# Softmax of the attention scores over sample and prompt columns together: one 768-wide maximum and sum for each head

## The chip, the cores and the metric

The kernel runs on one core of a Trainium2 chip. The metric is device time in microseconds (us) of one execution, lower is better; the kernel before has a median of 1966.47 us in three runs (1965.4 to 1966.96). Engines are named as in the profile: PE (TensorE, matrix multiply), DVE (VectorE), ACT (ScalarE), POOL (GpSimd), SP (SyncE, which issues most transfers).

## The reference

A trunk of two layers. Each layer runs three token mixers on the same normalised input and merges them; sample (512 tokens) and prompt (256 tokens) are two independent sequences that share all weights, so attention never crosses from one to the other.

```python
def encoder_layer(x, c_act, ...):
    h = rmsnorm(x, g_pre) * (1 + scale) + shift
    z = h @ w_in                                      # 1024 -> 8864 columns
    o_a = mla_attention(cq, ckv, kr, ...)             # A: 8 heads, dense
    o_b = dilated_attention(rope(q), rope(k), v)      # B: 3 dilations x 4 heads, joined to 4
    o_c = neighbourhood_attention(q, k, v, rpb)       # C: 8 heads, window of 8 x 16 on a grid
    p_a = (o_a * silu(gate_a)) @ w_pa                 # the same for b, c
    mixed = mg[0] * p_a + mg[1] * p_b + mg[2] * p_c   # mg = sigmoid(merge)
    return x + gate * rmsnorm(mixed @ w_out, g_post)
# the middle of each attention
    p = softmax(q k^T * scale [+ bias, masked])
    o = p v
```

## The kernel before

**Layout.** Activations lie feature-major: partitions are features, the T = 768 columns are tokens, sample in columns 0 to 511 and prompt in 512 to 767 (GROUPS in the code). Matrix products run on operands split into a rounded `hi` and a rest `lo`, each in a 4-byte rounded type: ACT casts `hi`, DVE (sometimes POOL) subtracts to get `lo`, and PE multiplies with both.

**One head.** Scores are computed transposed: keys on the partitions, queries in the columns. The score tiles of a head are four `tq` tiles of 128 x 768 (128 keys each); the sample has four key tiles (columns 0 to 511 of all four), the prompt two (columns 512 to 767 of the first two). PE writes score parts to PSUM, ACT copies them (branch A, L647) or DVE adds bias and mask (branch C, L992 to L994; branch B, L825 and L830) into `tq`. The softmax needs a maximum and a sum over keys, that is over the tiles and over the partitions: DVE combines the tiles elementwise (L662, L664), and POOL reduces over the 128 partitions and hands the result to all of them (`partition_all_reduce`, L665; in branch B L853 and L868). Then DVE subtracts the maximum (L670), ACT exponentiates in place (L671), ACT and DVE make `hi` (L679) and `lo` (L680), and PE multiplies with the values (L683, into `o_ps`). The sum is reduced in the same way and sent to DRAM by SP (L672); it divides the output later (`row_gains`), so the multiplication with the values does not wait for it. All this stood once for the sample and once for the prompt: `soft_keys` is called for each of them in branches A and C, and branch B has its own loop (L840 to L869).

**Order.** Each engine works its instructions in the order of its own list. A list scheduler puts them in that order at build time and also decides when buffers are reused, so a change of a few instructions moves others. In the attention branches PE has other products to do between the heads' parts: projections of the layer's input that are needed later (`gate`, and `mg` for the merge). These are called fillers below. A head's scores go out, then some fillers, then the product with the values. PE in its order waits where the softmax of a head is not yet done.

**Buffers.** The scratch tiles of 512 columns come from a ring (`s`, 6 slots x 512, tiles given out in turn by `S()`); the softmax's tile of combined scores and its reduced result, the diagonal of `rows_of` (L226), branch C's bias tile `bp` and two tiles of the output projection (L1148) use it.

**Merge.** Behind branch C, `hi` and `lo` of the branches' outputs are made (`hi<-ox` on ACT at L247, `lo<-ox` through `sub_lo` at L160, on DVE, every third on POOL). The first of them already stand among the last heads of branch C. The library that POOL's `partition_all_reduce` needs is loaded over anew when an elementwise operation has stood between two of them; the listed order shows such a load as a row `ISA` without operands.

Of the kernel before, what the change touches and what calls it, by code (L numbers as in the profile page):

```python
# [20 lines left out]
P = 128  # L21
D = 1024
KT = 8
# [43 lines left out]
def trunk_kernel(ctx, tc, x_t, c_row, c_col, w_ada0, w_ada, cols, w_a, w_feat, w_val, w_val2, w_uqk, w_qr, w_uv, w_pj, w_o,  # L67
# [12 lines left out]
    BUFS = dict(ta=8, tm=4, tq=8, wo=18, cv=14, gp=2, xt=3, ut=3, st=11, rp=5, go=5, f=1, dn=1)  # L80


    RINGS = dict(q=(4, 1024), wh=(4, NS), wl=(4, NS), s=(6, NS), wr=(3, 1024), z=(16, 4), z4=(4, 2 * KT), nv=(8, 12))
    SINGLE = dict(hm=2 * KT * T, pz=NPZ * 2 * NS, rope=2 * NS, ident=P, ones=P, mb=1152, col=depth * NCOL,
                  ada=depth * 48, ada2=depth * 96, gpost=depth * 16, ab=depth * KT * 4, row=P)
    ROUNDED = ("hm", "pz", "q", "wh", "wl")
# [139 lines left out]

    def rows_of(y, bc, eng=None, dg=None):

        dg = S() if dg is None else dg
# [33 lines left out]


    nc.sync.dma_start(out=col, in_=cols)
    zero = S()
    nc.vector.memset(zero, 0.0)
    for z2 in pz:
        for z in z2:
# [11 lines left out]
        return out  # L281

    spare = []
    wide = [part["rope"], part["mb"][:, :1024], part["s"][:, 2048:]]

    def ada_load(src, j, tag, rest, n):

# [290 lines left out]
    def branch_a(l, h_, h):  # L578
# [14 lines left out]
        for pr in range(4):  # L593
# [37 lines left out]
            for e in range(2):  # L631
                hd = (pr % 2) * 2 + e
                (qs, qrs), ka = qn[e], kn[e]
                prods = ((ka, qs), (kb[e], qs), (krs, qrs))
                tq = [U("tq") for _ in range(4)]
                for g, (o, n) in enumerate(GROUPS):
                    nk = n // P

                    for k0 in range(0, nk, 1 + g):
                        sp = SP()  # L640
                        for k in range(1 + g):
                            kc = slice(o + (k0 + k) * P, o + (k0 + k + 1) * P)
                            for j, (w, a) in enumerate(prods):
                                nc.tensor.matmul(sp[:, k * 256:k * 256 + n], w[:, kc], a[:, o:o + n],
                                                 start=(j == 0), stop=(j == 2))
                        for k in range(1 + g):
                            nc.scalar.copy(tq[k0 + k][:, o:o + n], sp[:, k * 256:k * 256 + n])  # L647
                for g, (o, n) in enumerate(GROUPS):
                    xs = [x[:, o:o + n] for x in tq[:n // P]]
                    soft_keys(xs, n, den_scr[l, pr, e, 0:1, o:o + n])  # L650
                    o_ps = ps_o.tile([P, NS], F32, tag="o", name="o_ps")[:, :n]
                    for k, x in enumerate(xs):
                        pv(x, [(o_ps, vslice(va, hd, o // P + k), lambda a: a)], k == 0, k == n // P - 1)
                    out_half(o_ps, o_t, e, [(lambda a: a[:, o:o + n], lambda a: a)])
            nc.vector.tensor_mul(o_t, o_t, row_gains(l, pr))
            finish_pair(l, pr, o_t, u)

    def soft_keys(xs, n, den):

        def across(op):  # L660
            out, red = (S(), S()) if n > 256 else halves(S())
            nc.vector.tensor_tensor(out, xs[0], xs[1], op=op)  # L662
            for x in xs[2:]:
                nc.vector.tensor_tensor(out, out, x, op=op)  # L664
            nc.gpsimd.partition_all_reduce(red, out, P, RED.max if op == ALU.max else RED.add)  # L665
            return red

        m = across(ALU.max)
        for x in xs:
            nc.vector.tensor_sub(x, x, m)  # L670
            nc.scalar.activation(x, x, AF.Exp)  # L671
        nc.sync.dma_start(out=den, in_=across(ALU.add)[0:1])  # L672

    def pv(x, terms, first, last):
# [113 lines left out]
    def branch_b(l, h, hl):  # L788
# [4 lines left out]
        for hd in range(4):  # L793
# [39 lines left out]
            for g, (o, n) in enumerate(GROUPS):  # L833
                nt = n // 128
                t0 = o // 128
                tbv = tbs[g]
                v1, v2 = (x.rearrange("p (s i) -> p s i", s=SB[g]) for x in tbv)

                def across(out, op):
                    nc.vector.tensor_tensor(strided(out[:, :n], g), v1, v2, op=op)  # L840
                    if g == 0:
                        nc.vector.tensor_tensor(out, out, tq[0][:, :NS], op=op)
                        for t in (1, 2):
                            ow = out[:, NW[t]:NW[t] + 256]
                            nc.vector.tensor_tensor(ow, ow, tq[1][:, (t - 1) * 256:t * 256], op=op)  # L845
                    else:
                        for w in wins:
                            nc.vector.tensor_tensor(out[:, :256], out[:, :256], w, op=op)

                mx = S()  # L850
                across(mx, ALU.max)
                m = S()
                nc.gpsimd.partition_all_reduce(m[:, :n], mx[:, :n], P, RED.max)  # L853
                if g == 0:
                    nc.vector.tensor_sub(tq[0][:, :NS], tq[0][:, :NS], m)
                    nc.vector.tensor_sub(two(tq[1][:, :NS]), two(tq[1][:, :NS]), win_ap(m))
                else:
                    for w in wins:
                        nc.vector.tensor_sub(w, w, m[:, :256])
                nm = strided(m[:, :n], g)  # L860
# [87 lines left out]
    def branch_c(l, h, hl):  # L948
        state["phase"] = "c"
        vcs = None  # L950
        for pr in range(4):
# [12 lines left out]
            for e in range(2):  # L964
# [3 lines left out]

                bm, bp = U("rp", name="bm"), S()
# [18 lines left out]
                for t in range(2):  # L990
                    edge = bm[:, 512 + t * P:640 + t * P]
                    nc.vector.tensor_add(tq[t][:, 0:P], sp[t][:, 0:P], edge)  # L992
                    nc.vector.tensor_add(tq[t][:, P:NS], sp[t][:, P:], bm[:, P - t * P:512 - t * P])
                    nc.vector.tensor_add(tq[t][:, NS:], sp[2][:, t * 256:t * 256 + 256], bp[:, t * 256:t * 256 + 256])  # L994
                for g, (o, n) in enumerate(GROUPS):
                    xs = [x[:, o:o + n] for x in tq]
                    soft_keys(xs, n, den_scr[l, 6 + pr, e, 0:1, o:o + n])
# [131 lines left out]
    def project(l, mixed, last):  # L1129
# [14 lines left out]
        for t in range(T // P):  # L1144
            g = int(t >= 4)
            c0 = t * P - GROUPS[g][0]
            xt = U("xt", name="xt"), S()
            x2, u2 = xt[1][:, :256], xt[1][:, 256:]  # L1148
# [263 lines left out]
```

## Time and profile before

| | before |
|---|---|
| median of 3 runs | 1966.47 us (1965.4 to 1966.96) |
| the profiled execution's own time, its span | 1966.35 us, 1964.6 us |
| busy: PE, DVE, ACT, POOL | 94%, 78%, 52%, 34% |
| mean granted clock of PE | 0.978 |
| `partition_all_reduce` at L665 | 128 instructions, 314.2 us |

"Busy" is the share of the span in which an engine works; the mean says little of a single stage. The stages in the span are: preparation to about 130 us, then in layer 0 branch A to 360, B to 600, C to 800, merge and output projection to 1060, and in layer 1 branch A from 1150, B from 1360, C from 1600 to about 1805, merge and output after it.

### The profile page before, as it was taken

The page shows a single profiled execution, that of the slowest core. Times are in us where ns is not written, and L with a number is a line of the kernel's source. Part 1 is how long each engine was busy: PE and PEld are TensorE (multiplying, and loading weights), DVE is VectorE, ACT ScalarE, POOL GpSimd, SP SyncE. Part 2 cuts the span into 40 slices and gives each one's busy share as a digit, 9 for nine tenths or more (in the row PEclk, how much of TensorE's full clock was granted, in tenths as well). Part 3 has the DMA queues.
Part 4 walks back from the last instruction along what each step waited for, and adds up shares of the span by engine and source line. Part 5 has one row for each costly group of instructions (what it writes and reads, how often), then busy time and mean ns, then how long its engine had stood idle before and what let it go on. Part 6 is the DMA issues. An engine that isn't in the chain of part 4 may idle for free. (4 is left out here: it accounts for less than half of the span.)

```text
span 1964.6 us, 30204 instructions
## 1 busy us (share of the span) xinstructions
PE 1845.0 (94%) x10674; PEld 1638.1 (83%) x10674; DVE 1530.9 (78%) x3018; ACT 1018.6 (52%) x2123; POOL 664.2 (34%) x432
## 2 busy tenths in 40 slices
PE   7897999999989987999999999999999999987998
PEld 6886888888877876888999888889888778876898
DVE  8957768579987999896587467687699868997763
ACT  5356556356577455322464356574566684653241
POOL 6404415202221454316534024253022212454570
PEclk9998999999999999999999999999999999998999
DMA  8432241232313233445452332422222222233652
GB/s 294 150 117 62 86 139 57 71 99 82 92 54 92 79 117 115 167 143 191 140 197 89 124 99 88 135 76 86 87 85 85 88 75 89 87 107 99 217 174 71
DMA packets 94904, 221.25 MB, mean 113 GB/s; under 512 B 18096, under 2 KB 32504, under 8 KB 94752
## 3 DMA queue, kind: packets, MB, share of 16 engines
q1 hardware_dynamic: 90144, 213.02, 33.4%
q10 hardware_dynamic: 4608, 6.29, 1.1%
q8 instruction: 84, 1.38, 0.3%
q14 instruction: 68, 0.56, 0.1%
HBM read 173.78 MB, written 28.18 MB: 103 GB/s over the span
## 5 line engine op out<-in xcount | busy, mean ns | idle before, releaser
L665 POOL PARTITION_ALL_REDUCE fixed<-fixed x128 | 314.2, 2486 | 496.3 <-DVE fixed L662 337.0
L201 PE MATMUL mg<-fixed 128*128 128x512 f32 (+1 forms) x2304 | 436.2, 342 | 1.4 <-DVE o_t L397 0.7
L201 PEld LDWEIGHTS mg<-fixed 128*128 128x128 f32 x2304 | 360.3, 191 | 51.6 <-PE sp L984 1.0
L177 ACT CAST fixed<-fixed 128x512 fp32r<-128x512 f32 (+1 forms) x332 | 199.5, 606 | 339.3 <-PE mg L201 117.8
L160 DVE TENSOR_TENSOR fixed<-fixed,fixed 128x512 fp32r<-128x512 f32 (+3 forms) x309 | 224.2, 729 | 113.9 <-ACT fixed L177 110.7
L201 PE MATMUL qkb<-fixed 128*128 128x512 f32 (+1 forms) x1152 | 211.9, 338 | 0.0
L201 PEld LDWEIGHTS qkb<-fixed 128*128 128x128 f32 x1152 | 177.0, 189 | 24.2
L201 PE MATMUL gate<-fixed 128*128 128x512 f32 (+1 forms) x960 | 184.0, 341 | 1.6 <-DVE tq L830 1.3
L201 PEld LDWEIGHTS gate<-fixed 128*128 128x128 f32 x960 | 150.0, 191 | 22.0 <-DVE tq L830 1.5
L1064 PE MATMUL pp<-hi,fixed 128*128 128x512 f32 (+1 forms) x640 | 161.5, 340 | 5.0 <-ACT th L1019 4.7
L680 DVE TENSOR_TENSOR fixed<-tq,fixed 128x512 fp32r<-128x512 f32 (+1 forms) x160 | 127.9, 821 | 2.7 <-ACT fixed L679 2.5
L1064 PEld LDWEIGHTS pp<-hi,fixed 128*128 128x128 f32 x640 | 111.9, 192 | 19.9 <-ACT th L1019 5.1
L671 ACT ACTIVATE tq<-tq 128x512 f32<-128x512 f32 (+1 forms) x160 | 83.4, 545 | 82.7 <-DVE tq L670 82.5
L429 POOL MEMSET kb<- 64x768 f32 x56 | 41.1, 736 | 209.5 <-PE sp L820 121.0
L670 DVE TENSOR_TENSOR tq<-tq,fixed 128x512 f32<-128x512 f32 (+1 forms) x160 | 97.8, 660 | 16.3 <-POOL fixed L665 16.2
L1163 PE MATMUL op<-wo,fixed 128*128 128x384 f32 (+1 forms) x648 | 108.2, 320 | 1.8 <-POOL wo L160 1.8
L1064 PE MATMUL pp<-lo,fixed 128*128 128x512 f32 (+1 forms) x320 | 108.9, 341 | 0.8 <-DVE lo L160 0.8
L1163 PEld LDWEIGHTS op<-wo,fixed 128*128 128x128 f32 x648 | 101.3, 188 | 3.2 <-POOL wo L160 3.1
L311 DVE SCALAR_TENSOR_TENSOR fixed<-tm,fixed 128x768 f32<-128x768 f32 (+1 forms) x128 | 93.3, 729 | 2.1 <-DMA tm<-in_w_ada_dram 0.4
L868 POOL PARTITION_ALL_REDUCE fixed<-fixed x16 | 49.0, 3084 | 128.4 <-DVE fixed L845 65.7
L662 DVE TENSOR_TENSOR fixed<-tq 128x256 f32<-128x256 f32 (+1 forms) x128 | 79.1, 623 | 14.3 <-ACT tq L647 10.8
L679 ACT CAST fixed<-tq 128x512 fp32r<-128x512 f32 (+1 forms) x160 | 80.8, 530 | 11.0 <-PE o_ps L683 8.2
(245 smaller groups left out, 3910.7 us busy)
## 6 DMA issues: line engine op xcount, KB each, us to landing
fixed<-in_w_feat_dram SPq DMA_DIRECT2D x108, 512.0 KB
th_scr<-the SPq DMA_DIRECT2D x35, 384.0 KB
th<-th_scr SPq DMA_DIRECT2D x35, 384.0 KB
tm<-in_w_ada_dram SPq DMA_DIRECT2D x32, 384.0 KB
fixed<-in_w_val_dram SPq DMA_DIRECT2D x20, 512.0 KB
xs<-xb SPq DMA_DIRECT2D x96, 96.0 KB
fixed<-in_w_pj_dram SPq DMA_DIRECT2D x32, 256.0 KB
fixed<-in_w_o_dram SPq DMA_DIRECT2D x16, 512.0 KB
```

The source lines that it names most:

```text
L160: eng.tensor_sub(out, a, b)
L177: nc.scalar.copy(hi[:, :m], raw[:, o:o + m])
L201: state["mm"] = nc.tensor.matmul(outs[g], w[:, wsl], a[g], start=(i == 0 and wi == 0), stop=(i == nk - 1 and wi == 2))
L311: nc.vector.scalar_tensor_tensor(junk, x, 1.0, c, ALU.mult, ALU.mult, accum_out=ada2[:, l, i, g, j:j + 1])
L662: nc.vector.tensor_tensor(out, xs[0], xs[1], op=op)
L665: nc.gpsimd.partition_all_reduce(red, out, P, RED.max if op == ALU.max else RED.add)
L670: nc.vector.tensor_sub(x, x, m)
L671: nc.scalar.activation(x, x, AF.Exp)
L679: nc.scalar.copy(hi, x)
L680: nc.vector.tensor_sub(lo, x, f(hi))
L1064: nc.tensor.matmul(pp, w[:, ws], o[k][a][:, o_:o_ + n], start=(i == 0), stop=(i == 3 * nk - 1))
L1163: mm = nc.tensor.matmul(op[cc], m[a][g][:, k, c0:c0 + P], parts[k][cc][b], start=(k == 0 and i == 0), stop=(k == KT - 1 and i == 2))
```

## The change

The maximum and the sum of a head are made once, over 768 columns: combined tile 128 x 768, one reduction over the partitions for the maximum, one for the sum. In branches A and C the subtraction and the exponential of the first two `tq` tiles are 768 wide, those of the last two 512. In branch B the combining and the subtraction stay in two parts (their windows differ), the exponentials are 768 wide, and both maxima are made before the first subtraction. The sum goes to DRAM in one transfer. The ring `s` has four slots of 768 columns (3072 columns as before), and its other users take the first 512 columns of a slot. In the changed kernel lines behind `soft_keys` are three or four further down: combining L665 and L667, reduction L668, subtraction L673, exponential L674, `hi` L682, `lo` L683, product with the values L686; branch B's reductions L851.

```diff
-    RINGS = dict(q=(4, 1024), wh=(4, NS), wl=(4, NS), s=(6, NS), wr=(3, 1024), z=(16, 4), z4=(4, 2 * KT), nv=(8, 12))
+    RINGS = dict(q=(4, 1024), wh=(4, NS), wl=(4, NS), s=(4, T), wr=(3, 1024), z=(16, 4), z4=(4, 2 * KT), nv=(8, 12))
...
+                soft_keys(tq, den_scr[l, pr, e, 0:1])
                 for g, (o, n) in enumerate(GROUPS):
                     xs = [x[:, o:o + n] for x in tq[:n // P]]
-                    soft_keys(xs, n, den_scr[l, pr, e, 0:1, o:o + n])
...
-    def soft_keys(xs, n, den):
+    def soft_keys(tq, den):
+
+
+        cols = (T, T, NS, NS)
 
         def across(op):
-            out, red = (S(), S()) if n > 256 else halves(S())
-            nc.vector.tensor_tensor(out, xs[0], xs[1], op=op)
-            for x in xs[2:]:
-                nc.vector.tensor_tensor(out, out, x, op=op)
+            out, red = S(), S()
+            nc.vector.tensor_tensor(out, tq[0], tq[1], op=op)
+            for x in tq[2:]:
+                nc.vector.tensor_tensor(out[:, :NS], out[:, :NS], x[:, :NS], op=op)
             nc.gpsimd.partition_all_reduce(red, out, P, RED.max if op == ALU.max else RED.add)
             return red
 
         m = across(ALU.max)
-        for x in xs:
-            nc.vector.tensor_sub(x, x, m)
-            nc.scalar.activation(x, x, AF.Exp)
+        for x, n in zip(tq, cols):
+            nc.vector.tensor_sub(x[:, :n], x[:, :n], m[:, :n])
+            nc.scalar.activation(x[:, :n], x[:, :n], AF.Exp)
         nc.sync.dma_start(out=den, in_=across(ALU.add)[0:1])
...
-                for x in tq:
-                    nc.scalar.activation(x[:, o:o + n], x[:, o:o + n], AF.Exp, scale=0.125)
-                sm = S()
-                across(sm, ALU.add)
-                dn = S()
-                nc.gpsimd.partition_all_reduce(dn[:, :n], sm[:, :n], P, RED.add)
-                nc.sync.dma_start(out=den_scr[l, 4 + hd // 2, e, 0:1, o:o + n], in_=dn[0:1, :n])
+            for x in tq:
+                nc.scalar.activation(x, x, AF.Exp, scale=0.125)
+            nc.sync.dma_start(out=den_scr[l, 4 + hd // 2, e, 0:1], in_=across(ALU.add)[0:1])
```

DVE's list at the first head of branch A, layer 0, before (`tq` are the score tiles, `fixed_73` the plain scratch, `fixed_72` the rounded scratch with `hi` and `lo`):

```order
L662 TENSOR_TENSOR fixed_73<-tq 128x512
L664 TENSOR_TENSOR fixed_73<-fixed_73,tq 128x512
L662 TENSOR_TENSOR fixed_73<-tq 128x256
L664 TENSOR_TENSOR fixed_73<-fixed_73,tq 128x512
L410 SCALAR_TENSOR_TENSOR qs<-qn_1721,qs 64x512
L410 SCALAR_TENSOR_TENSOR qs<-qn_1722,qs 64x256
L670 TENSOR_TENSOR tq<-tq,fixed_73 128x256 x2
L662 TENSOR_TENSOR fixed_73<-tq 128x256
L670 TENSOR_TENSOR tq<-tq,fixed_73 128x512 x4
L662 TENSOR_TENSOR fixed_73<-tq 128x512
L680 TENSOR_TENSOR fixed_72<-tq,fixed_72 128x512
```

The same place of the changed kernel:

```order
L665 TENSOR_TENSOR fixed_73<-tq 128x768
L410 SCALAR_TENSOR_TENSOR qs<-qn_1703,qs 64x512
L410 SCALAR_TENSOR_TENSOR qs<-qn_1704,qs 64x256
L667 TENSOR_TENSOR fixed_73<-fixed_73,tq 128x512 x2
L673 TENSOR_TENSOR tq<-tq,fixed_73 128x768 x2
L673 TENSOR_TENSOR tq<-tq,fixed_73 128x512 x2
L665 TENSOR_TENSOR fixed_73<-tq 128x768
L683 TENSOR_TENSOR fixed_72<-tq,fixed_72 128x512
```

The prompt's separate combining (128x256) and its two subtractions are gone into rows of 128x768, and two operations on `qs` (the next head's queries) stand inside the combining for the maximum instead of behind it.

POOL's list at the last heads of branch C, layer 1, before (an `ISA` row with sizes is a reduction, one without is a load of the library):

```order
L429 MEMSET kb 64x768 x2
L665 ISA fixed_73<-fixed_73 128x256
L665 ISA fixed_73<-fixed_73 128x512
L665 ISA fixed_73<-fixed_73 128x256
L160 ISA
L160 TENSOR_TENSOR lo<-ox,hi 128x768
L665 ISA
L665 ISA fixed_73<-fixed_73 128x512
L665 ISA fixed_73<-fixed_73 128x256
L665 ISA fixed_73<-fixed_73 128x512 x2
L665 ISA fixed_73<-fixed_73 128x256 x2
```

The same place of the changed kernel:

```order
L429 MEMSET kb 64x768 x2
L668 ISA fixed_73<-fixed_73 128x768 x2
L160 ISA
L160 TENSOR_TENSOR lo<-ox,hi 128x768
L668 ISA
L668 ISA fixed_73<-fixed_73 128x768 x5
```

Before, the `lo` stands behind the last sum of the sixth head and ahead of the seventh's maxima; now it stands between the sixth head's maximum and its sum.

PE's list at the second head of branch A, layer 0, before (`o_ps` are the products with the values, `sp` the scores, `gate` and `mg` the fillers):

```order
L683 MATMUL o_ps<-fixed_72,va 128x512 x8
L644 MATMUL sp<-qs,ka 128x256
L644 MATMUL sp<-qs,kb 128x256
L644 MATMUL sp<-qrs,krs 128x256
...
L683 MATMUL o_ps<-fixed_72,va 128x256 x4
L201 MATMUL gate_1798<-fixed_72 128x512 x22
L201 MATMUL gate_1799<-fixed_72 128x256 x22
L683 MATMUL o_ps<-fixed_72,va 128x512
```

The same place of the changed kernel, just ahead of that head's product with the values:

```order
L201 MATMUL mg_1841<-fixed_72 128x512
L201 MATMUL mg_1842<-fixed_72 128x256
L686 MATMUL o_ps<-fixed_72,va 128x512 x5
L686 MATMUL o_ps<-fixed_72,va 128x256
L686 MATMUL o_ps<-fixed_72,va 128x512 x3
L686 MATMUL o_ps<-fixed_72,va 128x256 x3
L201 MATMUL mg_1900<-fixed_72 128x512 x19
L201 MATMUL mg_1901<-fixed_72 128x256 x19
```

Now all 24 pairs of `gate` and the first 24 pairs of `mg` stand between this head's scores and its first `o_ps`; before, 22 pairs of `gate` did.

## Rows read from the trace of the kernel before

**Rows 1.** The page, part 1: busy time of each engine, share of the span.

```profile
PE 1845.0 (94%) x10674; PEld 1638.1 (83%) x10674; DVE 1530.9 (78%) x3018; ACT 1018.6 (52%) x2123; POOL 664.2 (34%) x432
```

**Rows 2.** PE's waits by line and releaser: us in total, times, longest.

```profile
PE o_ps L683 <- DVE fixed L680: 16.1, 16, 2.1
PE o_ps L683 <- ACT tq L647: 11.2, 1, 11.2
PE o_ps L683 <- ACT fixed L679: 8.4, 2, 6.1
```

**Rows 3.** Windows inside branch C, layers 0 and 1: PE, PEld, DVE, ACT, POOL busy; clock.

```profile
680.00:780.00 100.00, 88.83 (x502) 76.41 (x502) 97.46 (x172) 52.43 (x108) 53.89 (x26) 0.95 0.34 112
1690.00:1765.00 75.00, 66.16 (x379) 56.13 (x378) 71.96 (x125) 44.85 (x95) 37.80 (x19) 0.98 0.30 97
```

**Rows 4.** Window: branch A, layer 0, columns as in rows 3.

```profile
130.00:360.00 230.00, 209.60 (x1154) 181.99 (x1153) 173.46 (x288) 132.29 (x286) 88.29 (x38) 0.95 0.29 92
```

**Rows 5.** POOL's timeline, single reductions: start, us, line, [idle before, releaser].

```profile
663.96 1.73 POOL L665 PARTITION_ALL_REDUCE fixed<-fixed  x1
686.75 1.06 POOL L665 PARTITION_ALL_REDUCE fixed<-fixed  x1 [1.23 <-DVE fixed L662]
1354.54 3.24 POOL L665 PARTITION_ALL_REDUCE fixed<-fixed  x1 [7.84 <-DVE fixed L664]
1770.72 1.80 POOL L665 PARTITION_ALL_REDUCE fixed<-fixed  x1 [10.19 <-DVE fixed L662]
```

**Rows 6.** DVE's groups by line and shape: 680 to 780, 1690 to 1765, whole span.

```profile
L662 DVE TENSOR_TENSOR fixed<-tq 128x512 f32<-128x512 f32 x11 | 7.4, 683 | 0.0
L670 DVE TENSOR_TENSOR tq<-tq,fixed 128x256 f32<-128x256 f32 x8 | 3.0, 416 | 0.0
L460 DVE TENSOR_TENSOR xb<-xb,xs 128x768 f32<-128x768 f32 x24 | 22.9, 952 | 0.2
L680 DVE TENSOR_TENSOR fixed<-tq,fixed 128x512 fp32r<-128x512 f32 x96 | 87.5, 925 | 0.1
```

**Rows 7.** Timelines of POOL, DVE and PE at the first head of branch A, layer 0.

```profile
158.88 3.11 POOL L665 PARTITION_ALL_REDUCE fixed<-fixed  x2 [40.12 <-DVE fixed L662]
159.29 1.01 DVE L410 SCALAR_TENSOR_TENSOR qs<-qn,qs 64x512 fp32r<-64x512 f32 x2
162.68 3.39 DVE L670 TENSOR_TENSOR tq<-tq,fixed 128x512 f32<-128x512 f32 x4
169.01 1.28 DVE L680 TENSOR_TENSOR fixed<-tq,fixed 128x512 fp32r<-128x512 f32 x2
170.41 2.08 PE L683 MATMUL o_ps<-fixed,va 128*128 128x512 f32 x4 [11.16 <-ACT tq L647]
```

**Rows 8.** Timelines of PE, ACT and POOL at the last heads of branch C, layer 1.

```profile
1767.77 4.17 PE L201 MATMUL mg<-fixed 128*128 128x512 f32 x16
1767.90 0.83 ACT L247 CAST hi<-ox 128x768 fp32r<-128x768 f32 x1 [3.79 <-DMA ox<-o_scr]
1774.09 0.83 ACT L247 CAST hi<-ox 128x768 fp32r<-128x768 f32 x1
1780.53 1.84 POOL L160 TENSOR_TENSOR lo<-ox,hi 128x768 fp32r<-128x768 f32 x1 [8.02 <-DVE fixed L690]
1788.33 2.87 POOL L665 PARTITION_ALL_REDUCE fixed<-fixed  x2 [5.96 <-issue]
1793.12 0.58 PE L683 MATMUL o_ps<-fixed,vb 128*128 128x256 f32 x1 [6.08 <-ACT fixed L679]
```

**Rows 9.** Window at the last heads of branch C, layer 1, columns as in rows 3.

```profile
1789.00:1806.10 17.10, 9.18 (x28) 7.46 (x29) 15.90 (x23) 8.04 (x17) 11.34 (x5) 0.50 0.21 65
```

**Rows 10.** DVE and POOL timelines in branch C; durations of line L680, ns min/median/max.

```profile
1737.82 2.73 DVE L680 TENSOR_TENSOR fixed<-tq,fixed 128x512 fp32r<-128x512 f32 x1
1737.39 3.60 POOL L665 PARTITION_ALL_REDUCE fixed<-fixed  x1 [3.97 <-DVE fixed L662]
L680 DVE TENSOR_TENSOR fixed<-tq,fixed x160: 403/677/2753, 166.6 to 1816.8; 128x512 fp32r<-128x512 f32 x96, 128x256 fp32r<-128x256 f32 x64
```

More of the change, by code (lines that the diff above doesn't have):

```diff
@@ L227, in rows_of @@
     def rows_of(y, bc, eng=None, dg=None):
-        dg = S() if dg is None else dg
+        dg = S()[:, :NS] if dg is None else dg
         for t in range(y.shape[-1]):
@@ L265, in trunk_kernel @@
     nc.sync.dma_start(out=col, in_=cols)
-    zero = S()
+    zero = S()[:, :NS]
     nc.vector.memset(zero, 0.0)
@@ L283, in trunk_kernel @@
     spare = []
-    wide = [part["rope"], part["mb"][:, :1024], part["s"][:, 2048:]]
+    wide = [part["rope"], part["mb"][:, :1024], part["s"][:, 2048:3072]]
     def ada_load(src, j, tag, rest, n):
@@ L832, in branch_b, with across @@
             early(l, hl, FILL[l][9 + hd])
[L833 to L840, printed above, removed]
+            def across(op):
+                both, red = S(), S()
+                for g, (o, n) in enumerate(GROUPS):
+                    v1, v2 = (x.rearrange("p (s i) -> p s i", s=SB[g]) for x in tbs[g])
+                    out = both[:, o:o + n]
+                    nc.vector.tensor_tensor(strided(out, g), v1, v2, op=op)
                     if g == 0:
@@ L847, in across @@
                         for w in wins:
[L848 to L853, printed above, removed]
+                            nc.vector.tensor_tensor(out, out, w, op=op)
+                nc.gpsimd.partition_all_reduce(red, both, P, RED.max if op == ALU.max else RED.add)
+                return red
+            ms = across(ALU.max)
+            for g, (o, n) in enumerate(GROUPS):
+                v1, v2 = (x.rearrange("p (s i) -> p s i", s=SB[g]) for x in tbs[g])
+                m = ms[:, o:o + n]
                 if g == 0:
@@ L858, in branch_b @@
                     for w in wins:
-                        nc.vector.tensor_sub(w, w, m[:, :256])
-                nm = strided(m[:, :n], g)
+                        nc.vector.tensor_sub(w, w, m)
+                nm = strided(m, g)
                 nc.vector.tensor_sub(v1, v1, nm)
                 nc.vector.tensor_sub(v2, v2, nm)
-                for x in tq:
-                    nc.scalar.activation(x[:, o:o + n], x[:, o:o + n], AF.Exp, scale=0.125)
-                sm = S()
-                across(sm, ALU.add)
-                dn = S()
-                nc.gpsimd.partition_all_reduce(dn[:, :n], sm[:, :n], P, RED.add)
-                nc.sync.dma_start(out=den_scr[l, 4 + hd // 2, e, 0:1, o:o + n], in_=dn[0:1, :n])
+            for x in tq:
+                nc.scalar.activation(x, x, AF.Exp, scale=0.125)
+            nc.sync.dma_start(out=den_scr[l, 4 + hd // 2, e, 0:1], in_=across(ALU.add)[0:1])
+            for g, (o, n) in enumerate(GROUPS):
+                nt = n // 128
+                t0 = o // 128
+                tbv = tbs[g]
                 o_ps = ps_o.tile([P, NS], F32, tag="o", name="o_ps")
@@ L967, in branch_c @@
                 prods = ((ka, qs), (kb[e], qs))
-                bm, bp = U("rp", name="bm"), S()
+                bm, bp = U("rp", name="bm"), S()[:, :NS]
                 nc.scalar.dma_start(out=bm[:, 512:], in_=bias_s[l, hd])
@@ L994, in branch_c @@
                     nc.vector.tensor_add(tq[t][:, NS:], sp[2][:, t * 256:t * 256 + 256], bp[:, t * 256:t * 256 + 256])
+                soft_keys(tq, den_scr[l, 6 + pr, e, 0:1])
                 for g, (o, n) in enumerate(GROUPS):
                     xs = [x[:, o:o + n] for x in tq]
-                    soft_keys(xs, n, den_scr[l, 6 + pr, e, 0:1, o:o + n])
                     o_ps = ps_o.tile([P, NS], F32, tag="o", name="o_ps")
@@ L1147, in project @@
             xt = U("xt", name="xt"), S()
-            x2, u2 = xt[1][:, :256], xt[1][:, 256:]
+            x2, u2 = xt[1][:, :256], xt[1][:, 256:NS]
             xt = xt[0]
```

## The prediction

> **What bounds the kernel now.** I read the page first: PE is busy in 94% of the span, DVE in 78%, POOL in 34% [rows 1]. The change takes nothing from PE: it issues as many matrix products as before. So it can only win or lose in the waits of PE, and the second view is the list of those waits. Three of its lines belong to the softmax: PE stands before the product with the values until `lo`, the evacuation of scores or `hi` is there, 16.1 us in 16 pieces, 11.2 us in one, 8.4 us in two [rows 2]. Third I asked, stage by stage, which engine is full when PE waits. In branch A of layer 0 nothing is: PE works 209.60 of 230 us and DVE 173.46 [rows 4]; its losses sit at single places, above all at the first head. In the middle of branch C it is DVE: 97.46 of 100 us in layer 0 and 71.96 of 75 us in layer 1, while PE works 88.83 and 66.16 [rows 3]. There a shorter DVE list should shorten the span; elsewhere only a shorter chain from the last score to the first product with the values does.
>
> **POOL.** Single reductions, matched by the listed order to their sizes, took 1.73 us (maximum, 512), 1.06 (maximum, 256), 3.24 (sum, 512) and 1.80 (sum, 256) [rows 5]. The line through the two sizes gives 1.73 + 0.67 = 2.40 us for a maximum over 768 and 3.24 + 1.44 = 4.68 for a sum. A head so costs 7.08 instead of 7.83 us, and 160 reductions become 80: 40 heads x 0.75 = 30 us less on POOL. POOL is no bound by its busy share [rows 1], so none of it counts by itself. What counts is when a result is there: a head's maximum comes 2.40 - 1.73 = 0.67 us later than the sample's alone did, and when the sum of the head ahead stands in front of it on POOL, another 3.24 -> 4.68, 1.44 us later.
>
> **DVE.** In A and C a head loses four instructions: one 512- and one 256-wide operation become one of 768, once in the maximum, once in the sum, twice in the subtraction. Undisturbed, the three widths take 0.683, 0.416 and 0.952 us [rows 6], so a merge saves 0.147 us and a head 0.59 us. Over 32 heads that is 19 us, but it is worth time only where DVE is full: the windows of rows 3 hold 11 combinings of 512 (two to a head, 5.5 heads) and 8 subtractions of 256 (two to a head, 4 heads) [rows 6]. 9.5 heads x 0.59 = **-5.5 us**. Bounds: 0, if the freed time goes into other waits of PE, and -5.5 x 16/9.5 = -9 if all of branch C's 16 heads gain. In branch B DVE's count stays; there only exponentials are merged, on ACT, which is busy in 52% [rows 1] of the span, as in A and C: nothing. If ACT were full anywhere, its 96 merged exponentials would count there as DVE's merges do; its share of 52 and 60% in the windows of rows 3 excludes it.
>
> **DVE beside POOL.** A `lo` of 512 took 2.73 us while a reduction of 3.60 us had begun just before it; the median over all widths is 0.677 and the mean of the 512-wide is 0.925 [rows 6, 10]. So some operations are held up to 2.05 us, most not at all. The excess, 4 x 0.25 = 1 us a head, over 9.5 heads 9.5 us, falls by 10% if it goes with the reductions' time and by half if it goes with their number: -1 to -5; I take **-2 us**, nearer the first, since the sums, which run beside the `lo`s, keep their length. The Trainium skill, "SBUF — State Buffer", section "Who interferes with whom", says that a DVE instruction with two SBUF inputs and a GpSimd instruction that reads SBUF exclude one another for a whole instruction; the row of 2.73 us fits it, the median does not. What that rule would make of the sum is a rival below.
>
> **First head of A, layer 0.** PE waits 11.16 us for it with no filler at hand, and its order there is the same after the change [rows 7]. Before, POOL has both maxima at 158.88 + 3.11 = 161.99. After, the 768-wide combining needs the prompt's scores too. Their own combining, 0.42 long, and a last one of 0.68 stood ahead of 159.29 [rows 7], so they were there by 158.2; I take 157.7, since DVE was busy with the sample before. 157.7 + 0.95 + 1.01 (the `qs` pair [rows 7], which now stands inside) + 2 x 0.68 = 161.0, plus 2.40 = 163.4, 1.4 us later. The subtractions then take 2 x 0.95 + 2 x 0.68 = 3.3 instead of 3.39 [rows 7]. Cost: **+1.3 us**, between 0 and +3.
>
> **Other heads of A.** I counted in the order how much work PE has between a head's last score and its first product with the values, at 0.25 us per 512 columns (16 took 4.17 us [rows 8]) and half for 256. In layer 0 that was 3.4, 8.5, 12.9, 22.9, 8.4, 18.5, 11.9 and 23.5 us; after the change it is 3.4, 17.9, 17.8, 28.0, 20.0, 27.7, 24.8 and 22.4. In layer 1 the lowest four rise from about 15 to above 20. So the scheduler has put the fillers ahead of the products that waited. The chain needs, on idle engines, 2.3 (combining) + 4.68 + 2.40 (a sum ahead, the maximum) + 3.3 (subtractions) and four more steps of 512 columns (evacuation, exponential, `hi`, `lo`) at about 0.68 [rows 10] = 15.4 us at the worst: less than 17.8. A has half of the 32 heads that share the 16.1 us of waits for `lo` [rows 2], so up to 8; as C is fuller I take less than half of that, **-3 us**, between 0 and -8. In branch B PE has 14.7 to 24.9 us before and 22 to 28.9 after: nothing; without that cover each of 8 heads would pay its later results, 0.67 + 1.44 us.
>
> **Last heads of C, layer 1.** Before, POOL makes a `lo` between reductions: it starts at 1780.53 after 8.02 us of idleness, and the next reduction only at 1788.33, after 5.96 us in which POOL waits for nothing that shows [rows 8]; the order has a load of the library on either side. The seventh head's maxima are done at 1788.33 + 2.87 = 1791.20, PE then stands for 6.08 us [rows 8], and in the 17.1 us from 1789 PE works 9.18 at a granted clock of 0.50, 1.2 GHz [rows 9]. At 2.4 GHz without waits this work takes 4.6: 12.5 us lost. After, `lo` stands one step earlier, between the sixth head's maximum and sum. It needs its `hi`, before done at 1774.9 [rows 8]. Another `hi` waited 3.79 us for its operand from DRAM until 1767.90 [rows 8]. If the `hi` in question comes without such a wait, by 1764, POOL is free at 1764 + 6 + 1.84 + 6 = 1778, and 7.1 us later, at 1785, sum and maximum are done; if it stands two steps behind a wait as long as that one, at about 1772, they are done at 1793. I take the middle, 1789: **-2 us**, between -6 and, with half the clock lost for it, +4.
>
> **The rest.** 80 transfers of sums become 40, issued by SP; they serve the division of a pair of heads, off the path, and half of SP's waits for POOL go with them. The ring holds one head in either form (6 x 512, 4 x 768). The output projection's two uses of it need the slot of four token tiles back instead of six; a 256-column load is all that hangs on it: nothing.
>
> **Sum.** From the profiled execution's 1966.35 us (its span of 1964.6 and 1.75 around it; 0.12 below the median): -5.5 - 2 + 1.3 - 3 - 2 = -11.2, **1955 us**.
>
> **Rivals.**
> *Slower, 1976.* One reduction over 768 columns in place of two that could be passed by. POOL works in order, so the next head's maximum waits 4.68 + 2.40 = 7.1 us behind a sum, not 3.24 + 1.73 = 5.0. It decides where DVE's own queue, three quarters full in A [rows 4], stretches the 15.4 us chain beyond PE's 18 to 28: 2.4 us more are enough at the shortest. Ten such heads cost 21 us; against the gains of 11 that is +10. For it: at the first head the 768-wide form is later. Against: the longer covers.
> *No change, 1966.* The waits for the softmax go, but PE then stands for the keys' preparation and the outputs' evacuation, which the same full DVE makes; the gain in C is nothing, the one in A balances the first head.
> *Far faster, 1936.* The longer covers take away all waits for `lo` and `hi`: 16.1 + 8.4 [rows 2] = 24.5 us, of which the sum holds 5; 19 more. Against: in C the waits are DVE's, and it remains nearly full.
> *The exclusion for whole instructions, 1948.* DVE is stopped whenever POOL reduces: POOL works 53.89 + 37.80 = 91.69 us in the two windows [rows 3], 10% less is -9 instead of -2. Against: the median of rows 10. The Trainium skill's rule cited above is this one.
>
> **How the numbers follow.** The forecast gets 0.44 (its own range 1946 to 1963), slower 0.21, no change 0.14, far faster 0.12, exclusion 0.09. The range 1934 to 1978 leaves out about half of the outermost cases on either side, some 0.17. 0.2% is 4 us, about what a measurement of this kernel can tell from no change. Faster by more than that: nine tenths of the forecast, the far faster and the exclusion, 0.61; within: the rest of the forecast and nearly all of no change, 0.16; slower: 0.23 with the tail of no change.
>
> **What would show it.** Reductions: 80 of them, 2.4 and 4.7 us alone. DVE: some 19 us less busy, and the middle of C some 0.6 us a head shorter with DVE still above 95%. First head: a wait near 12.5 us. A: fewer waits for `lo`. End of C: seventh maximum done near 23 us after the sixth head's last exponential, a shorter wait. The prediction is wrong if PE's waits at the product with the values grow in A or B (the rival of the single sum), if DVE's saving in C shows up as waits of PE for keys, or if the library is loaded at another head where PE has less to do.

## The result, and the profile after

The changed kernel takes 2001.5 us (median of 4 runs, 2000.19 to 2003.13), the kernel before 1965.93 beside it: ratio 1.0178, 95% interval 1.0164 to 1.0192. It is 35 us slower; 1955 was forecast. The page of the profiled execution after (span 1999.3 us), busy time of each engine:

```profile
PE 1861.4 (93%) x10674; PEld 1652.7 (83%) x10674; DVE 1527.1 (76%) x2890; ACT 1009.6 (50%) x2027; POOL 604.1 (30%) x352
```

DVE has the 128 instructions less that were counted, but only 3.8 us less work than in [rows 1]; POOL is relieved by 60 us, twice the 30 that were forecast. The list of PE's waits after, against [rows 2]:

```profile
PE o_ps L686 <- DVE fixed L683: 34.7, 20, 5.6
PE o_ps L686 <- DVE tq L998: 12.5, 1, 12.5
PE o_ps L686 <- ACT tq L647: 12.4, 1, 12.4
```

The waits of the product with the values for `lo` have doubled, from 16.1 to 34.7 us. The 12.4 is the first head of branch A; the 12.5 stands at the end of branch C in layer 1, where 6.08 stood before. Where the time went is told by windows from branch C's first score product to its last product with the values, layers 0 and 1 (columns: window, length, busy PE, PEld, DVE, ACT, POOL, clock, DMA share, GB/s). Before:

```profile
641.60:801.60 160.00, 144.11 (x830) 125.55 (x829) 151.44 (x268) 85.49 (x176) 78.07 (x38) 0.96 0.33 109
1648.00:1818.70 170.70, 151.98 (x863) 131.34 (x862) 153.91 (x269) 85.02 (x176) 78.31 (x39) 0.93 0.29 94
```

After:

```profile
649.40:830.50 181.10, 152.57 (x836) 132.89 (x835) 159.31 (x236) 83.14 (x159) 69.37 (x22) 0.88 0.29 91
1674.30:1857.30 183.00, 152.69 (x867) 132.41 (x866) 156.05 (x241) 83.39 (x162) 70.60 (x23) 0.92 0.30 92
```

The two pairs of windows hold about as many products (1693 and 1703). Branch C became 21.1 and 12.3 us longer, 33 of the 35. PE stands 28.5 instead of 15.9 us in layer 0 and works at a granted clock of 0.88 instead of 0.96. Read DVE's column against the window's length: idle for 8.6 and 16.8 us before, 21.8 and 26.9 after. The engine that was to be relieved is no longer full, and the branch is slower all the same. Outside branch C the balance is small: it begins 7.8 us later in layer 0 (649.4 for 641.6), and the rest gives some 6 us back.

### The profile page after: what moved, and what is told of

The parts are those of the page before. It is cut to its first block, busy times and chain, and to the rows that moved or that the text cites. A ratio compares the mean times of both kernels' runs of the same rounds, so it can differ in the third digit from the quotient of the medians.

```text
span 1999.3 us, 29739 instructions
## 1 busy us (share of the span) xinstructions
PE 1861.4 (93%) x10674; PEld 1652.7 (83%) x10674; DVE 1527.1 (76%) x2890; ACT 1009.6 (50%) x2027; POOL 604.1 (30%) x352
## 4 chain that ended last, share of the span: by engine, by line
PE 44%; DVE 9%; ACT 2%; DMA 2%; issue 2%; SPq 0%; POOL 0%; DVEq 0%; ACTq 0%; POOLq 0%
PE mg L201 12%; PE pp L1068 8%; PE op L1167 7%; PE qkb L201 4%; PE gate L201 2%; DVE fixed L683 2%; PE sp L644 1%; DVE fixed L160 1%; PE cq L554 1%; PE vp L756 1%; PE o_ps L686 1%; PE qc L201 1%; PE ck L554 1%; DVE qs L410 1%; DMA den<-rden_scr 1%
## 5 line engine op out<-in xcount | busy, mean ns | idle before, releaser
L201 PE MATMUL mg<-fixed 128*128 128x256 f32 (+1 forms) x2304 | 434.1, 342 | 7.7 <-ACT the L1023 3.4
L668 POOL PARTITION_ALL_REDUCE fixed<-fixed x64 | 266.8, 4179 | 537.7 <-DVE fixed L667 283.6
L160 DVE TENSOR_TENSOR fixed<-fixed,fixed 128x512 fp32r<-128x512 f32 (+3 forms) x309 | 235.6, 766 | 142.7 <-ACT fixed L177 138.0
L851 POOL PARTITION_ALL_REDUCE fixed<-fixed x16 | 62.3, 3892 | 222.7 <-DVE fixed L847 86.1
L683 DVE TENSOR_TENSOR fixed<-tq,fixed 128x512 fp32r<-128x512 f32 (+1 forms) x160 | 119.7, 773 | 2.7 <-ACT fixed L682 2.6
L674 ACT ACTIVATE tq<-tq 128x768 f32<-128x768 f32 (+1 forms) x96 | 74.0, 775 | 65.8 <-DVE tq L673 62.5
L311 DVE SCALAR_TENSOR_TENSOR fixed<-tm,fixed 128x768 f32<-128x768 f32 (+1 forms) x128 | 97.4, 761 | 2.4 <-POOL fixed L279 0.5
L673 DVE TENSOR_TENSOR tq<-tq,fixed 128x768 f32<-128x768 f32 (+1 forms) x96 | 94.8, 1039 | 4.6 <-POOL fixed L668 4.5
L686 PE MATMUL o_ps<-fixed,vb 128*128 128x256 f32 x192 | 42.0, 327 | 49.0 <-DVE fixed L683 30.9
L396 ACT COPY o_t<-o_ps 64x512 f32<-64x512 f32 (+3 forms) x96 | 54.6, 592 | 61.1 <-PE o_ps L686 35.8
```

The lines of the kernel that those rows point to most:

```text
L160: eng.tensor_sub(out, a, b)
L201: state["mm"] = nc.tensor.matmul(outs[g], w[:, wsl], a[g], start=(i == 0 and wi == 0), stop=(i == nk - 1 and wi == 2))
L311: nc.vector.scalar_tensor_tensor(junk, x, 1.0, c, ALU.mult, ALU.mult, accum_out=ada2[:, l, i, g, j:j + 1])
L673: nc.vector.tensor_sub(x[:, :n], x[:, :n], m[:, :n])
L674: nc.scalar.activation(x[:, :n], x[:, :n], AF.Exp)
L683: nc.vector.tensor_sub(lo, x, f(hi))
```

## The experiments

Four theories were put to the test in turn. **1**: DVE stands behind the division's way through DRAM. **2**: the softmax in one piece is too long a chain. **3**: the 768-wide sum stops DVE and POOL. **4**: heads wait in a ring, because the prompt bias of branch C takes the slot of the maximum of the head ahead. In the edits, `-` is the changed kernel unless the kernel before is named. "In two parts" means sample and prompt apart, as before, but in columns of the same four 768-wide slots, in the order maximum, subtraction and exponential, sum, values.

**c_split and a_split.**

```diff
-                soft_keys(tq, den_scr[l, 6 + pr, e, 0:1])
+                run = soft_split(tq)          # mo, mr, so, sr = S(), S(), S(), S()
                 for g, (o, n) in enumerate(GROUPS):
+                    run(g, den_scr[l, 6 + pr, e, 0:1])   # max, sub, exp, sum of columns o:o+n
```

> The changed kernel with branch C's softmax in two parts again (sample, then prompt: two maxima, two sums, two transfers of sums), on the changed kernel's 768-wide tiles; A and B stay merged. All theories that put the loss into branch C expect its 33 us back: 1962 to 1972. If the loss came from the ring of four slots or from A and B, it stays near 2001.

> The changed kernel with branch A's softmax in two parts again, B and C merged. Branch C's loss stays: about 2000. If merging in A hurts what follows it, below 1990.

1975.07 us (ratio 1.0042, 1.0027 to 1.0056) and 1997.73 (1.0155, 1.0139 to 1.017). Merging branch C costs 26 us; putting A in two parts gives back 4, so A's merge is not what makes the loss. The expectations wanted 1962 to 1972 of c_split: not all of the loss is in branch C. The windows of branch C in two parts:

```profile
649.70:804.30 154.60, 137.72 (x795) 120.01 (x794) 149.36 (x266) 82.64 (x172) 78.71 (x38) 0.93 0.35 105
1654.50:1820.80 166.30, 147.79 (x842) 126.58 (x840) 152.47 (x265) 84.51 (x176) 76.55 (x39) 0.97 0.31 97
```

DVE is idle for 5.2 and 13.8 us here, and full again in layer 0. These windows hold 66 products fewer than the changed kernel's (1637 for 1703: fillers stand elsewhere), so the 26 us are read from the times and not from the windows' lengths.

**after_nodiv and before_nodiv**: no `row_gains` and no multiplication in branch C.

```diff
-            den = row_gains(l, 6 + pr)
...
-                    nc.vector.tensor_mul(d, d, sv(den[:, o:o + n]))
             finish_pair(l, 6 + pr, o_t, u)
```

> The changed kernel without the division of branch C's outputs by the sums (the reductions and the transfers of the sums to DRAM stay; the reciprocal, its way through DRAM and the multiplication are left out, so branch C's output is not normalised). Theory 1, DVE stands behind the division's way through DRAM: its 24 us of waits go, with part of the lost clock: 1970 to 1980. Theory 2, the one-piece chain is too long for PE's cover: only the multiplications' own 16 us of DVE go, partly: above 1990. Theory 3, DVE is stopped by the 768-wide sum: above 1990.

> The kernel before without the division of branch C's outputs (the same part left out). Its DVE waited less than 4 us for the division in branch C: theory 1 expects 1955 to 1963. Theories 2 and 3 expect the same gain as in the changed kernel without the division.

1996.3 us (1.0155, 1.0127 to 1.0184) and 1956.35 (0.9942, 0.9926 to 0.9958). The reason for theory 1 was this list of DVE's waits in the changed kernel, 650 to 830 us:

```profile
DVE o_t L1016 <- DMA den<-rden_scr: 8.5, 3, 5.3
DVE fixed L160 <- ACT fixed L177: 5.6, 4, 2.4
```

The waits are there, but without the division the changed kernel gains 5 us and the kernel before 12, so that the two lie 40 us apart instead of 35. Theory 1 falls: the wait is a place where the loss shows, not its cause. The largest wait of the changed kernel in branch C is such a place; DVE and PE at the end of the branch, layer 1:

```profile
1824.35 1.58 DVE L1016 TENSOR_TENSOR o_t<-o_t,den 128x448 f32<-128x448 f32 x3 [5.12 <-DMA den<-rden_scr]
1829.38 0.68 DVE L683 TENSOR_TENSOR fixed<-tq,fixed 128x512 fp32r<-128x512 f32 x1
1830.97 1.41 PE L686 MATMUL o_ps<-fixed,vb 128*128 128x256 f32 x5 [12.45 <-DVE tq L998]
```

The `lo` (L683) stands in DVE's list behind the division (L1016), which itself waits 5.12 us for its operand.

**c_sumsplit, parsplit**: branch C's sum in two parts; every reduction of A and C in two.

```diff
+            for o, n in GROUPS:               # c_sumsplit
+                across(so, sr, ALU.add, o, n)
...
-            nc.gpsimd.partition_all_reduce(red, out, P, RED.max if op == ALU.max else RED.add)
+            for o, n in GROUPS:               # parsplit
+                nc.gpsimd.partition_all_reduce(red[:, o:o + n], out[:, o:o + n], P, RED.max if op == ALU.max else RED.add)
```

> The changed kernel with branch C's sum in two parts (combining, reduction, transfer for sample and prompt apart), maximum, subtraction and exponential merged. Theory 3, it is the long sum that stops DVE and POOL: back to about 1975. Theory 4, it is the merged maximum: 1990 to 2005. Theory 2 lies between, 1985.

> The changed kernel with each reduction over the partitions in branches A and C done in two, 512 and 256 columns, everything on DVE and ACT merged as in the changed kernel. Theory 3: most of the loss back, about 1975. Theories 2 and 4: the slot is still free only when the prompt's scores are in the combined maximum: 1990 to 2010.

2000.88 us (1.0172, 1.0156 to 1.0187) and 1999.42 (1.0165, 1.015 to 1.018). The time doesn't come back, so theory 3 doesn't explain the loss as a whole. It may hold for a part. The windows of branch C in parsplit:

```profile
656.20:828.90 172.70, 144.65 (x811) 125.83 (x810) 154.51 (x235) 80.44 (x156) 74.24 (x38) 0.89 0.31 97
1679.50:1853.50 174.00, 153.40 (x866) 132.61 (x864) 147.69 (x236) 83.71 (x161) 80.70 (x39) 0.92 0.30 95
```

With the reductions in two, DVE is busy for 302.2 us in branch C instead of 315.4, and the windows are 17.4 us shorter, with 26 products fewer; but branch C begins 6.8 us later (656.2 for 649.4), as branch A's reductions were split too. So some of branch C's loss, perhaps 10 us, can hang on the long reductions. Nor does either edit change that on POOL the sum of one head stands ahead of the maximum of the next. What is left of the merge in both is one combined maximum, subtraction and exponential. The maximum in two parts beside a merged sum was not tried.

**nolo**: `LO_POOL` without its entry `m=3`, so that no library is loaded between reductions.

> The changed kernel with every lo of the merge on DVE, none on POOL, so that no library is loaded between the reductions of branch C's last heads. The wait of 12.45 us before the seventh head's product in layer 1 has such a load ahead of it: if the load makes it, 1988 to 1995; if the ring of theory 4 alone makes it, 1997 to 2004.

2001.6 us (1.0173, 1.0158 to 1.0188): no effect on the time, though the wait of 12.45 us has such a load ahead of it and is 9.7 us here.

**before_rot** and **c_swap** change only which scratch slot is taken when. **bias_sp** has the prompt bias loaded by SP.

```diff
+                pm = halves(S())              # before_rot, ahead of sm: the prompt's maximum second
...
+            if swap and op == ALU.max:        # c_swap
+                out, red = red, out
...
-                nc.scalar.dma_start(out=bp, in_=bias_p[l, hd])
+                nc.sync.dma_start(out=bp, in_=bias_p[l, hd])
```

> The kernel before with nothing changed but the order in which a head of branch C takes its scratch slots: the prompt's maximum second, so that the next head's prompt bias goes into the slot of the prompt's maximum, no longer into that of the sample's. Theory 4, head after head waits in a ring: prompt bias, prompt scores, maximum over them, slot free, next head's prompt bias (in the kernel before the bias takes the slot of the sample's maximum, which needs no prompt score; in the changed kernel the one maximum needs them all): slower by 15 to 35 us, 1981 to 2001. Theories 2 (a longer chain from scores to values) and 3 (DVE stopped by the 768-wide sum): no difference, 1963 to 1972.

> The changed kernel with the prompt bias's load issued by SP in place of ACT. In the changed kernel's trace ACT issues it 1.5 to 4.6 us after the maximum that frees its slot. Theory 4: up to that time back in most of 14 heads, 10 to 30 us, unless SP itself stands behind another wait: 1972 to 1991. Theory 2: 1998 to 2005.

> The changed kernel with two slots of branch C exchanged and nothing else: the combined maximum and its reduced result change places, so that the next head's prompt bias takes the slot of the reduced maximum, which is free only when the subtractions have read it, 7 to 10 us after the reduction in the trace. Theory 4, the loop through the bias's slot sets the pace of the heads: each of some 14 heads is that much later, 30 us or more in all: above 2025. If the loop doesn't set the pace: 1997 to 2006.

1966.34 us (1.0, 0.999 to 1.001), 1998.98 (1.0163, 1.0146 to 1.0179) and 2004.01 (1.0202, 1.0177 to 1.0228). An earlier issue gains 2.5 us and a later release of the slot costs 2.5, both within what these runs can tell, where theory 4 wanted at least 10 and 30: the slot does not set the pace of the heads.

**after_btq, csplit_btq**: the bias loaded into the score tiles, merged and in two parts. **after_nobias, before_nobias, csplit_nobias**: no learned prompt bias.

```diff
-                bm, bp = U("rp", name="bm"), S()[:, :NS]
...
+                    nc.scalar.dma_start(out=tq[t][:, NS:], in_=bias_p[l, hd][:, t * 256:t * 256 + 256])
+                    nc.vector.tensor_add(tq[t][:, NS:], tq[t][:, NS:], mc[:, 512 + t * 256:768 + t * 256])
...
+                bm, bp = U("rp", name="bm"), mc[:, 512:1024]      # nobias: the mask alone
```

> The changed kernel with the prompt bias of branch C loaded straight into the prompt columns of the score tiles, mask added there, no slot of the ring taken; otherwise the same work (two mask additions of 256 instead of one of 512). Theory 4, head after head waits in a ring for the bias's slot: the loop is cut, most of the 33 us of branch C comes back: 1965 to 1980. Theory 2, the chain from scores to values is too long for PE's cover: 1998 to 2005.

> The control for the bias loaded into the score tiles: the changed kernel with branch C in two parts and the bias in the score tiles. Theory 4: in two parts the sample's softmax never stood in the ring of bias and maximum, so the move of the bias gains nothing: 1970 to 1980, as branch C in two parts alone (1975). If the bias in the score tiles were simply the better place, it gains the same 17 us as in the merged form: below 1963.

> The changed kernel without the prompt's learned bias in branch C (no load, no addition of the mask to it; the mask alone is added to the prompt's scores). Theory 4: no loop, 0.7 us of DVE less for each of 16 heads as well: 1958 to 1975. Theory 2: only what the kernel before gains by the same omission: 1988 to 1998.

> The kernel before without the prompt's learned bias in branch C, as the control. In it the bias is loaded into the slot of the sample's maximum, free early: only DVE's 16 x 0.7 us where it is full: 1955 to 1965 by both theories.

> The changed kernel with branch C in two parts and without the prompt's learned bias: the control for the merged kernel without it (1992.5), on the same ring. Theory 4, without the bias's slot the merge costs nothing: 1987 to 1997, the rest being the ring with one head's tiles in it. Theory 2, the one-piece chain costs by itself too: 1965 to 1977.

| branch C (A and B merged, same ring) | in two parts | merged |
|---|---|---|
| bias in the ring | 1975.07 (1.0042) | 2001.5 (1.0178) |
| no bias | 1971.56 (1.0029, 1.0013 to 1.0045) | 1992.45 (1.0133, 1.0107 to 1.0159) |
| bias in the score tiles | 1986.97 (1.0097, 1.0082 to 1.0112) | 1984.69 (1.009, 1.0073 to 1.0106) |

before_nobias: 1967.38 us (1.0002, 0.9991 to 1.0012), where 1955 to 1965 was expected. The first line gives the merge 26 us, the second 21, the third -2. In the second no bias stands in any slot, and nearly the whole cost is there: theory 4 falls but for a few us. The third line had looked like its proof; but there it is the two-part kernel that became 12 us slower by the move (1970 to 1980, or below 1963, was expected), for a reason that these runs don't show. And the merged kernel with the bias in the score tiles is 8 us faster than the one with no bias, which has less to do. So the order that the scheduler makes can move the time by about 10 us, and the merge's 20 to 26 us are known no better than that. The windows of branch C without bias, in two parts:

```profile
647.50:799.30 151.80, 133.04 (x770) 114.15 (x768) 146.44 (x254) 79.75 (x168) 74.56 (x38) 0.98 0.28 91
1652.70:1818.80 166.10, 147.61 (x832) 126.28 (x831) 150.06 (x260) 82.95 (x175) 77.75 (x39) 0.95 0.27 87
```

and merged:

```profile
650.00:815.80 165.80, 138.59 (x767) 119.30 (x766) 144.97 (x224) 78.67 (x154) 64.47 (x22) 0.91 0.28 89
1669.20:1840.50 171.30, 152.62 (x839) 131.37 (x838) 151.14 (x228) 80.97 (x159) 67.48 (x23) 0.92 0.26 82
806.19 0.58 PE L686 MATMUL o_ps<-fixed,vb 128*128 128x256 f32 x1 [10.17 <-DVE o_t L397]
```

The products are nearly as many (1602 and 1606), so the lengths can be compared here: 19.2 us more. With the merge DVE is idle for 41.0 instead of 21.4 us and PE for 45.9 instead of 37.3; the other 10.6 us are PE's products at a lower granted clock (0.91 and 0.92 for 0.98 and 0.95). The last line is one wait of PE at the last head of layer 0: it alone is longer than the whole difference in PE's idle time, so the loss isn't spread evenly over the heads.

**a_only, abc_split, btq_bsplit**: only A merged; nothing merged, on the ring of four slots; B in two parts beside after_btq. The edit is that of c_split, in branch B with the kernel before's lines.

> The changed kernel with only branch A merged, B and C in two parts on the ring of four 768-wide slots. Each merge costs by itself, C 26 us, B some 6, A nothing: 1964 to 1972. If A's merge has the gain that the prediction gave it (3 us less 1.3): 1961 to 1966.

> All three branches in two parts, on the changed kernel's ring of four 768-wide slots: the kernel before but for where its scratch lies. If the ring's shape itself costs, 1972 or more; if not, 1963 to 1970.

> The changed kernel with the bias in the score tiles and branch B's softmax in two parts again (A and C merged). PE's lost time in branch B of layer 0 is 6 us above that of the kernel before in every run with B merged: it comes back, 1974 to 1982. If it belongs to what A leaves behind, no change: 1983 to 1987.

1973.23 us (1.0035, 1.0024 to 1.0045), 1974.37 (1.0037, 1.0026 to 1.0049) and 1992.45 (1.0123, 1.0106 to 1.014). With nothing merged the new place of the scratch alone costs 8 us. Its window up to branch C's first score product in layer 0, the kernel before first:

```profile
0.00:641.60 641.60, 586.87 (x3354) 518.35 (x3355) 501.80 (x956) 368.25 (x754) 198.09 (x136) 0.97 0.34 107
0.00:651.30 651.30, 593.48 (x3354) 522.23 (x3355) 503.79 (x956) 368.76 (x754) 199.79 (x136) 0.96 0.34 106
```

The instructions are the same in number on every engine, and the time is 9.7 us longer: the ring's cost stands ahead of branch C in layer 0, and it is why branch C began 7.8 us later in the changed kernel. On this ring A's merge is worth 1 us and B's costs nothing (c_split, which has both, is within 2 us of both); in btq_bsplit B in two parts even costs 8. The expectation that B's merge costs 6 was a miss.

So the 35 us are 8 for the ring and its sharing, about nothing for A and B, and 26 for branch C. No complete version beat the kernel before. Of the theories the second is left, but it was not right everywhere: it expected 1985 of c_sumsplit and 1998 to 2005 of after_btq.

## Why the prediction was wrong

**The step that failed** is the paragraph on DVE: "-5.5 us" in branch C, between 0 and -9. The merge in branch C costs 26 us instead (c_split), and DVE, 97% busy before, is idle for 48.7 us in its two windows, where it was 25.4. The step took a full engine for one that is short of throughput, so that work taken from it must come back as time. before_nobias tests just that on the kernel before; its page:

```profile
PE 1841.8 (94%) x10674; PEld 1633.6 (83%) x10674; DVE 1522.9 (78%) x3002; ACT 1016.0 (52%) x2123; POOL 660.2 (34%) x432
```

DVE has 16 operations and 8.0 us less than in [rows 1], all of them in branch C, and the time stays (1.0002). (before_nodiv, with 11.8 us less on DVE, is 12 us faster, but there waits for DRAM go with the work.) The prediction also set the longer way of the merged maximum against PE's work only in branch A ("needs the prompt's scores too", +1.3 at the first head), not in branch C. The third head of branch C in layer 0 shows that way. (A head of branch C has two score tiles, not four, so the combining is one operation.) Before, timelines of DVE, POOL and PE:

```profile
676.76 0.54 DVE L993 TENSOR_TENSOR tq<-sp,bm 128x384 f32<-128x384 f32 x1
682.59 0.68 DVE L662 TENSOR_TENSOR fixed<-tq 128x512 f32<-128x512 f32 x1
683.20 0.68 DVE L974 TENSOR_TENSOR bm<-bm,fixed 128x512 f32<-128x512 f32 x1
683.43 2.09 POOL L665 PARTITION_ALL_REDUCE fixed<-fixed  x1 [0.34 <-POOL fixed L665]
693.26 0.39 PE L683 MATMUL o_ps<-fixed,vb 128*128 128x256 f32 x1
```

After:

```profile
685.43 0.54 DVE L997 TENSOR_TENSOR tq<-sp,bm 128x384 f32<-128x384 f32 x1
688.36 1.95 DVE L683 TENSOR_TENSOR fixed<-tq,fixed 128x512 fp32r<-128x512 f32 x4
688.53 6.92 POOL L668 PARTITION_ALL_REDUCE fixed<-fixed  x1 [12.07 <-DVE fixed L665]
690.84 0.74 DVE L998 TENSOR_TENSOR tq<-sp,fixed 128x256 f32<-128x256 f32 x2
691.50 3.21 DVE L978 TENSOR_TENSOR bm<-bm,fixed 128x512 f32<-128x512 f32 x1
695.30 0.95 DVE L665 TENSOR_TENSOR fixed<-tq 128x768 f32<-128x768 f32 x1
696.41 2.54 POOL L668 PARTITION_ALL_REDUCE fixed<-fixed  x1 [0.96 <-POOL fixed L668]
707.39 0.39 PE L686 MATMUL o_ps<-fixed,vb 128*128 128x256 f32 x1
```

From the end of the sample's last score addition to the start of its maximum over the partitions it was 6.1 us, and is 10.4: the maximum now needs the prompt's additions (L998), which come 4.9 us behind the sample's, and an operation for the next head stands on DVE ahead of the combining (L978). That operation took 3.21 us (0.68 at L974 before), beside the 768-wide sum of the head ahead; and POOL itself was not free before that sum ended at 695.45. So at this head the long sum has its part, by holding DVE and by standing ahead on POOL. To the first product it was 16.0 us and is 21.4. Over the eight heads, from the last score product to the first product with the values on PE's timeline, the mean is 28.7 us before, 27.6 in c_split and 37.7 after in layer 0 (26.2, 25.1 and 34.1 in layer 1). That PE then stands, that its granted clock is lower and that DVE idles is seen in the windows.

That the length of this chain is the cause is not shown. The same mean is 23.1 us in csplit_nobias and 26.7 in after_nobias in layer 0, 23.6 and 25.9 in layer 1: shorter with the merge than in the kernel before, and still 21 us between the two. Between the changed kernel and after_nobias it differs by 11.0 and 8.2 us a head, for 9 us of time in all. So the mean does not set the time. Whether it is the longer chain at the single heads where PE has no other work left, or another feature of the order that the scheduler made, stays open: every run is also a new order, and the move of the bias changed the time by 12 us the one way and 17 the other. A merged kernel in the order of the two-part one was not run.

**Term by term.** First head of A: +1.3 forecast, and PE's row reads 12.37 for the 11.16 of [rows 7]:

```profile
172.09 1.65 PE L686 MATMUL o_ps<-fixed,va 128*128 128x512 f32 x3 [12.37 <-ACT tq L647]
```

The reductions, 2.40 and 4.68 us forecast from the two sizes of [rows 5], were sized well: the maxima took some 2.50, the shorter of the sums 4.68, and others 5.04 and more:

```profile
673.95 2.50 POOL L668 PARTITION_ALL_REDUCE fixed<-fixed  x1 [0.93 <-POOL kb L429]
1756.31 4.68 POOL L668 PARTITION_ALL_REDUCE fixed<-fixed  x1 [10.10 <-DVE fixed L665]
666.40 5.04 POOL L668 PARTITION_ALL_REDUCE fixed<-fixed  x1 [8.20 <-DVE fixed L665]
```

The other heads of A, -3: -1 by a_only against abc_split, +4 by the changed kernel against a_split, so no gain that the runs can tell. "The rest ... nothing" for the ring: +8, the second step that failed; the paragraph looked at the output projection, and the cost stands in the branches ahead of C. The last heads of C, -2: the wait there doubled, and nolo shows that the library load, on which the term was built, doesn't matter for the time. Less holding of DVE by POOL, -2: DVE's busy time is 10 us longer than on the page of c_split, with 64 instructions fewer, so neither the saving nor the holding went as forecast in branch C:

```profile
PE 1854.3 (94%) x10674; PEld 1643.8 (83%) x10674; DVE 1517.2 (77%) x2954; ACT 1011.6 (51%) x2059; POOL 619.1 (31%) x384
```

**The rivals**: *slower, 1976* had the right sign, but named POOL's order behind the long sum, in branch A; a_split shows that the loss isn't there. In branch C that order is seen at single heads, as above, and no run took it away by itself: c_sumsplit and parsplit only show that the length of a single reduction isn't the whole. *No change* was right in one thing: DVE's saving in C ended in other waits. *Far faster* and *the exclusion* had the wrong sign.

## What to carry to other kernels

Here two short chains that pass the engines one behind the other were worth more than one chain with fewer instructions, even where an engine was 97% busy: before counting a merged instruction as gain, ask which of its inputs comes last, and what used to run while that input was awaited. Price it at every place where the merged step stands, above all where PE has little other work left, and not only at the first. Where a scheduler places everything anew, put the change in one branch at a time and change the buffers alone as a control: here the buffers alone cost 8 us.

## What the hardware showed that was not expected

In two rows DVE was held by a reduction on POOL, longer by the wider one. DVE's and POOL's timelines after:

```profile
734.18 4.15 DVE L665 TENSOR_TENSOR fixed<-tq 128x768 f32<-128x768 f32 x1
733.76 5.04 POOL L668 PARTITION_ALL_REDUCE fixed<-fixed  x1 [12.28 <-DVE fixed L665]
```

The same combining takes 0.95 us undisturbed (above, at 695.30), so it was held for 3.2 of the 5.04 us; in [rows 10] it was 2.05 of 3.60. The Trainium skill, "SBUF — State Buffer", section "Who interferes with whom", has the later of the two blocked for the whole of the other's instruction. The two rows show some 60% of it. Not every operation beside a reduction is held: in the third head above, four `lo`s (L683) took 1.95 us together at the start of the sum of 6.92 us, and only L978 behind them was held. And DVE's busy time fell by 3.8 us, where 128 instructions fewer had been counted as 19: what it lost to the reductions did not fall with their number (160 to 80).
